# An encoder layer on one core: four pairs of seven per block instead of three, and their recombination as accumulating DMAs on GpSimd's queue

## The chip, the core and the metric

The kernel runs on one core of one Trainium2 chip. A core has TensorE (PE in the rows, with its weight loads as PEld), VectorE (DVE), ScalarE (ACT), GpSimd (POOL) and SyncE (SP), and 16 DMA engines that move data for the queues of SP, ACT and POOL. The metric is the device time of one execution in microseconds (us), and the time of a kernel is the median of its runs. Lower is better.

## What is computed

One layer: a feed-forward half step, a mixing stage (a Fourier branch and a recurrent branch, gated and merged), a second feed-forward half step, and a final RMS norm. All data are float32, 256 positions of 2048 features, and the inner width of the feed-forward is 5632. The change concerns the two feed-forwards:

```
def swiglu(h, w_gate, w_up, w_down):
    return (jax.nn.silu(h @ w_gate) * (h @ w_up)) @ w_down
...
h = rms_norm(x, ffn1_norm[l])
x = x + FFN_RES_SCALE * swiglu(h, ffn1_w_gate[l], ffn1_w_up[l], ffn1_w_down[l])
...
h = rms_norm(x, ffn2_norm[l])
x = x + FFN_RES_SCALE * swiglu(h, ffn2_w_gate[l], ffn2_w_up[l], ffn2_w_down[l])
```

## The kernel before

**Precision.** A float32 operand is split into a high part (ACT casts it, `whi` at line 157) and a low part (DVE subtracts, `wlo` at line 158). A product then takes three matmuls: high by high, high by low, low by high.

**Gate/up.** Each feed-forward first computes gate and up in 11 blocks (NB) of 512 columns. A block walks over the 2048 input features in 8 pairs of 256; each pair needs one chunk of 1 MB of weights, four tiles of 128x512 (up and gate, two halves of 128 features each). The four output banks of a block are gate and up for two halves of the 256 positions. A pair is done in one of two ways. With **eight** products (24 matmuls of 512 columns) it needs only the four tiles' high and low parts. With **seven** products (Strassen's scheme in Winograd's form, 21 matmuls) it needs sums and differences of the weight tiles (`t13`, `t24` and their high and low parts, lines 172 to 190, nine buffers) and of the activations (`sm`, from `Norm.sums`). The seven products go to seven PSUM banks (P1 to P7), which at the end of a block are copied out by ACT (line 390, into `ga`, `gd`, `gb`, `gc`, `xt`) and then **recombined** by five additions on DVE (lines 398 to 404). SiLU (ACT, lines 402 and 406), the product gate times up (DVE, lines 407 and 409), and eight transposes on PE with a copy and a store on ACT's DMA queue (`turn`, lines 413 to 421: `gt`, then `dn`) follow. Of the 11 blocks the first has no seven, the other ten have three, in the order E S E S E S E E (E for eight, S for seven).

**Order.** Weights are prepared two pairs ahead (LOOK = 2): while PE works on pair n, ACT and DVE prepare pair n + 2. The recombination of block b - 1 stands in the program behind the preparation in pairs 1 to 4 of block b (`combine(b - 1, n - 1)`, lines 463 and 464), and its `turn` in pair 1 of block b + 1. Inside a feed-forward `keep_order` holds every engine to the program's order.

**Buffers.** The pool `unit` (30 buffers of 4 KB a partition) holds the activations, `sm`, `ga` to `gc`, and all tiles of the preparation by seven; a tile takes over the buffer of a tile that was released, and waits for the last reader of that one. Raw weights have three buffers (`raw`), loaded by SP in order; a load waits until the preparation of the chunk that held the buffer is done. The residual `x` has 16 KB a partition of its own.

**Down.** Then comes the down projection over 88 groups of 8 weight tiles. Its input G is read back from DRAM (`gf`, SP's queue, line 475) and split (lines 298 and 299) during the first 22 groups, two groups for each block of gate/up; the recombination of the last block is run there too, by the hooks `ahead(t)` at groups 2t:

```
dn_hooks = dict(dn_hooks) | {2 * t: ahead(t) for t in range(NB)}
```

## Time and profile before

| | |
|---|---|
| median of 3 runs | 1980.38 us (1977.99 to 1981.15) |
| the profiled execution's own time | 1980.42 us |
| its span in the trace | 1978.6 us |
| PE busy | 1959.8 us, 99% of the span |
| DVE, ACT, POOL busy | 1464.2, 1145.8, 0.2 us |
| granted TensorE clock, mean | 0.996 |
| DMA | 400.80 MB, mean 203 GB/s |

The span runs from the first to the last instruction that the trace shows; the time has 1.8 us more, for what lies around it. A matmul's end is modelled, so the busy share of PE is not its efficiency; the time from one start to the next is what counts.

### The profile page before, as it was taken

To read this page: it belongs to the slowest core of one execution; us is meant where nothing else is said; L and a number is where in the kernel's file an instruction comes from. 1 tells how busy PE (TensorE), PEld (TensorE's weight loads), DVE (VectorE), ACT (ScalarE), POOL (GpSimd) and SP (SyncE) were. 2 spreads that over 40 slices of the span, in tenths; PEclk is the share of its full clock that TensorE was granted. 3 is DMA by queue.
4 is the path that set the end of the run, shared out by engine and by line. 5 is a ranking of instruction groups with operands and counts; after the bars stand their busy time and mean duration, and the time that the engine had idled before them with its cause. 6 is when DMAs were issued, how large, how long until landed. Compare 5 with 4: busy or idle time off the path is not lost.

```text
span 1978.6 us, 25578 instructions
## 1 busy us (share of the span) xinstructions
PE 1959.8 (99%) x10196; PEld 1679.7 (85%) x10196; DVE 1464.2 (74%) x1657; ACT 1145.8 (58%) x1491; POOL 0.2 (0%) x4
## 2 busy tenths in 40 slices
PE   9999999999999999999999999999999999999997
PEld 7888888888888888898888888888888888888887
DVE  7898888888665557755886767778888888855454
ACT  7666566666554445558965555566656666654442
POOL 0000000000000000000000000000000000000000
PEclk9999999999999999999999999999999999999998
DMA  7666566666754555445555555646656666665462
GB/s 266 208 211 217 199 209 215 212 212 235 266 211 154 215 189 200 171 170 183 182 190 190 192 191 187 218 170 213 202 203 213 219 217 213 238 242 211 153 222 94
DMA packets 61143, 400.80 MB, mean 203 GB/s; under 512 B 7008, under 2 KB 7648, under 8 KB 16352
## 3 DMA queue, kind: packets, MB, share of 16 engines
q1 hardware_dynamic: 57168, 387.04, 56.5%
q10 hardware_dynamic: 3856, 12.13, 1.5%
q8 instruction: 79, 1.29, 0.3%
q14 instruction: 40, 0.33, 0.0%
HBM read 385.52 MB, written 13.63 MB: 202 GB/s over the span
## 4 chain that ended last, share of the span: by engine, by line
PE 96%; DVE 2%; ACT 1%; issue 0%; DMA 0%; SPq 0%; DVEq 0%; ACTq 0%
PE ps L448 45%; PE ps L227 31%; PE ps L232 17%; PE ps L417 1%; PE ps L229 1%; PE ps L230 1%; DVE lo L187 0%; DVE wlo L158 0%; ACT whi L157 0%; PE ps L692 0%; DMA x<-xT 0%; DVE x L901 0%; DVE gb L400 0%; DVE ga L398 0%; PE ps L705 0%
## 5 line engine op out<-in xcount | busy, mean ns | idle before, releaser
L158 DVE TENSOR_TENSOR wlo<-raw,whi 128x1024 fp32r<-128x1024 f32 (+1 forms) x589 | 702.2, 1220 | 318.2 <-ACT whi L157 317.4
L157 ACT CAST whi<-raw 128x1024 fp32r<-128x1024 f32 (+1 forms) x589 | 596.8, 1047 | 349.6 <-PE ps L227 260.3
L448 PE MATMUL ps<-whi,m 128*128 128x512 f32 x1856 | 583.4, 390 | 1.2 <-ACT whi L157 1.1
L448 PEld LDWEIGHTS ps<-whi,m 128*128 128x128 f32 x1856 | 349.1, 188 | 74.4 <-ACT whi L157 1.9
L448 PE MATMUL ps<-wlo,m 128*128 128x512 f32 x928 | 362.1, 390 | 0.5 <-DVE wlo L158 0.5
L227 PE MATMUL ps<-G,whi 128*128 128x512 f32 x1320 | 332.7, 394 | 4.8 <-ACT whi L157 4.0
L227 PEld LDWEIGHTS ps<-G,whi 128*128 128x128 f32 x1320 | 237.9, 189 | 49.1 <-ACT whi L157 4.6
L227 PE MATMUL ps<-m,whi 128*128 128x512 f32 x896 | 225.4, 393 | 0.0
L448 PEld LDWEIGHTS ps<-wlo,m 128*128 128x128 f32 x928 | 174.5, 188 | 37.4 <-DVE wlo L158 1.1
L232 PEld LDWEIGHTS ps<-G,wlo 128*128 128x128 f32 x1408 | 191.9, 191 | 13.0
L232 PE MATMUL ps<-G,wlo 128*128 128x256 f32 x1408 | 196.8, 283 | 0.0
L227 PEld LDWEIGHTS ps<-m,whi 128*128 128x128 f32 x896 | 160.9, 189 | 28.5
L182 ACT CAST t24h<-t 128x1024 fp32r<-128x1024 f32 x60 | 63.3, 1055 | 123.3 <-DVE t L178 123.3
L232 PEld LDWEIGHTS ps<-m,wlo 128*128 128x128 f32 x896 | 122.2, 190 | 8.4
L232 PE MATMUL ps<-m,wlo 128*128 128x256 f32 x896 | 125.6, 282 | 0.0
L448 PE MATMUL ps<-bh,m 128*128 128x512 f32 x240 | 95.1, 396 | 0.0
L187 DVE TENSOR_TENSOR lo<-t,t24h 128x1024 fp32r<-128x1024 f32 x60 | 73.3, 1221 | 21.7 <-ACT t24h L182 21.7
L448 PE MATMUL ps<-t13h,sm 128*128 128x512 f32 x240 | 83.7, 389 | 0.0
L187 DVE TENSOR_TENSOR lo<-raw,bh 128x1024 fp32r<-128x1024 f32 x60 | 73.1, 1219 | 0.0
L187 DVE TENSOR_TENSOR lo<-t,t13h 128x1024 fp32r<-128x1024 f32 x60 | 73.1, 1219 | 0.0
L176 DVE TENSOR_TENSOR t<-raw 128x1024 f32<-128x1024 f32 x60 | 73.1, 1218 | 0.0
L448 PE MATMUL ps<-lo,m 128*128 128x512 f32 x180 | 70.4, 391 | 0.1
(207 smaller groups left out, 2098.5 us busy)
## 6 DMA issues: line engine op xcount, KB each, us to landing
raw<-gu SPq DMA_DIRECT2D x171, 1024.0 KB, 4.9
raw<-dn SPq DMA_DIRECT2D x88, 1024.0 KB, 5.1
raw<-gates_w SPq DMA_DIRECT2D x34, 1024.0 KB, 4.9
raw<-win SPq DMA_DIRECT2D x24, 1024.0 KB, 5.0
raw<-proj SPq DMA_DIRECT2D x16, 1024.0 KB, 4.9
raw<-wout SPq DMA_DIRECT2D x16, 1024.0 KB, 4.9
dn<-gt ACTq DMA_DIRECT2D x22, 512.0 KB, 3.6
gf<-dn SPq DMA_DIRECT2D x22, 512.0 KB, 6.3
```

The lines of the kernel that those rows point to most:

```text
L157: ACT.copy(hi[:, a:b, :], src[:, a:b, :])
L158: DVE.tensor_tensor(lo[:, a:b, :], src[:, a:b, :], hi[:, a:b, :].bitcast(F32), ALU.subtract)
L176: DVE.tensor_tensor(t13, r[:, 0:4:3, :], r[:, 1::-1, :], ALU.subtract)
L182: ACT.copy(t24h, t24)
L187: DVE.tensor_tensor(lo, src, hi.bitcast(F32), ALU.subtract)
L227: PE.matmul(o[:, 0:512], lhsT=w, rhs=mv(0, 512), start=first, stop=False)
L229: PE.matmul(o[:, 0:256], lhsT=w, rhs=mv(0, 256), start=first, stop=False)
L230: PE.matmul(o[:, 0:256], lhsT=w, rhs=mv(256, 512), start=False, stop=False)
L232: PE.matmul(o[:, 0:256], lhsT=lo[:, t * P:(t + 1) * P], rhs=mv(0, 256), start=False, stop=last)
L417: PE.transpose(o[:, j // 2, 256 * (j % 2) + P * h:256 * (j % 2) + P * (h + 1)], g[:, h, P * j:P * (j + 1)], ident)
L448: PE.matmul(bank[o], lhsT=lhs, rhs=rhs, start=o not in begun, stop=left[o] == 0 and k == 2)
```

## The change

- `SPLIT` goes from three to four pairs of seven in each block but the first, and the order of a block becomes E S E S E S E S, so that a block ends with a seven. In every block but the first of each feed-forward one pair of 24 matmuls becomes one of 21.
- The five additions of the recombination leave DVE and become five DMAs on POOL's queue with an accumulating add (`add_to`): one operand is read, and added to the target in SBUF. The third reads what the first wrote, the fourth and the fifth read what the third wrote.
- The recombination now starts in pair 0 of the next block, in five steps instead of four; SiLU stays in pairs 2 and 3.
- `x` loses its own memory and becomes four tiles of the pool `unit`, which goes from 30 to 35 buffers. `x.put` writes it to DRAM at pair 6 of the second gate/up, and `x.get` is given to the down projections as a hook at group 14.
- `Norm.sums(3)` of the first feed-forward moves from pair 16 to pair 8.

```
--- before.py
+++ after.py
@@ -26,7 +26,7 @@
 
 NB = F // 512
 
-SPLIT = [0] + [3] * 10
+SPLIT = [0]+[4]*10
 
 
 GROUPS_DN = [(2, 4)] + [(1, KF)] * (KD // 2 - 2)
@@ -75,14 +75,13 @@
 
     const = ctx.enter_context(tc.tile_pool(name="const", bufs=1))
     wraw = ctx.enter_context(tc.tile_pool(name="wraw", bufs=3))
-    unit = ctx.enter_context(tc.tile_pool(name="unit", bufs=30))
+    unit = ctx.enter_context(tc.tile_pool(name="unit", bufs=35))
     wspl = ctx.enter_context(tc.tile_pool(name="wspl", bufs=8))
     work = ctx.enter_context(tc.tile_pool(name="work", bufs=2))
     psum = ctx.enter_context(tc.tile_pool(name="psum", bufs=4, space=bass.MemoryType.PSUM))
     dram = ctx.enter_context(tc.tile_pool(name="dram", bufs=1, space=bass.MemoryType.DRAM))
 
 
-    x = const.tile([P, KD, T], F32, name="x")
     pr = const.tile([P, NPAR], F32, name="pr")
     ones = const.tile([P, P], F32, name="ones")
     DVE.memset(ones, 1.0)
@@ -94,6 +93,33 @@
 
     def unit_tile(dt, shape=(P, 2, 512), name="u"):
         return unit.tile(list(shape), dt, tag="u", name=name)
+
+    class Residual:
+
+
+        def __init__(self):
+            self.new()
+
+        def new(self):
+            self.tiles = [unit_tile(F32, (P, 4, T), name="x") for _ in range(KD // 4)]
+
+        def __getitem__(self, key):
+            p, k, t = key
+            if isinstance(k, int):
+                return self.tiles[k // 4][p, k % 4, t]
+            assert k.start // 4 == (k.stop - 1) // 4
+            return self.tiles[k.start // 4][p, k.start % 4:k.start % 4 + k.stop - k.start, t]
+
+        def put(self, to):
+            for i, t in enumerate(self.tiles):
+                SP.dma_start(to[:, 4 * i:4 * i + 4, :], t)
+
+        def get(self, src):
+            self.new()
+            for i, t in enumerate(self.tiles):
+                SP.dma_start(t, src[:, 4 * i:4 * i + 4, :])
+
+    x = Residual()
 
     def new_ps():
         return psum.tile([P, 2, 512], F32, tag="ps", name="ps")
@@ -361,7 +387,7 @@
 
         def combine(b, n):
             g = late[0](n)
-            if n == 3:
+            if n == 4:
                 late.pop(0)
                 ready.append((b, g))
 
@@ -376,8 +402,8 @@
                 def rest(step):
                     if step < 2:
                         ACT.activation(a[:, step, :], a[:, step, :], AF.Silu, scale=norm.cols[:, step:step + 1])
-                    if step > 1:
-                        i = step - 2
+                    if step > 2:
+                        i = step - 3
                         DVE.scalar_tensor_tensor(g[:, i, :], d[:, i, :], norm.cols[:, i:i + 1], a[:, i, :], ALU.mult, ALU.mult)
                     return g
                 return evict, rest
@@ -389,20 +415,24 @@
             def evict(n):
                 ACT.copy(to[n], bank[n])
 
+            def add_to(o, t):
+                nc.gpsimd.dma_start(o, t, accum_op=ALU.add)
+
             def both(t):
                 return t.to_broadcast([P, 2, 512])
 
             def rest(step):
 
                 if step == 0:
-                    DVE.tensor_tensor(a, a, both(g[:, 0:1, :]), ALU.add)
-                    DVE.tensor_tensor(xt, xt, c[:, 1, :], ALU.add)
-                    DVE.tensor_tensor(g, c, both(a[:, 1:2, :]), ALU.add)
+                    add_to(a, both(g[:, 0:1, :]))
+                    add_to(xt, c[:, 1, :])
+                    add_to(c, both(a[:, 1:2, :]))
                 elif step == 1:
+                    add_to(d, c)
+                    add_to(xt, c[:, 0, :])
+                elif step == 2:
                     ACT.activation(a[:, 0, :], a[:, 0, :], AF.Silu, scale=R[:, 0:1])
-                    DVE.tensor_tensor(d, d, g, ALU.add)
-                    DVE.tensor_tensor(xt, xt, g[:, 0, :], ALU.add)
-                elif step == 2:
+                elif step == 3:
                     ACT.activation(d[:, 0, :], d[:, 0, :], AF.Silu, scale=R[:, 1:2])
                     DVE.scalar_tensor_tensor(g[:, 0, :], d[:, 1, :], R[:, 0:1], a[:, 0, :], ALU.mult, ALU.mult)
                 else:
@@ -460,8 +490,8 @@
                     del full[:k]
                 prep_upto(q + LOOK, lambda: empty(EARLY))
                 empty(8)
-                if b and 0 < n < 5:
-                    combine(b - 1, n - 1)
+                if b and n < 5:
+                    combine(b - 1, n)
         return lambda n: combine(NB - 1, n), lambda: turn(*ready.pop(0))
 
     def ffn(gu_nm, dn_nm, norm, after, cols_at, hooks={}, last=None, dn_hooks={}):
@@ -486,9 +516,9 @@
 
         def ahead(t):
             def run():
-                if t < 4:
+                if t < 5:
                     combine(t)
-                if t in (1, 4):
+                if t in (1, 5):
                     turn()
                 load_g(t + 2)
                 split_g(t + 1)
@@ -841,10 +871,10 @@
         return lambda: [f(j) for j in js]
     hooks = {0: each(n1.moving, [2, 3]), 1: each(n1.moving, [4, 5]), 2: each(n1.moving, [6]), 3: each(n1.moving, [7]),
              4: each(n1.square, range(3)), 5: each(n1.square, range(3, 6)), 6: each(n1.square, range(6, 8)),
-             7: lambda: ACT.dma_start(ident, eye), 16: each(n1.sums, [3])}
+             7: lambda: ACT.dma_start(ident, eye), 8: each(n1.sums, [3])}
     hooks |= {k: (lambda k=k, h=h: (h(), n1.sums(k - 3))) for k, h in list(hooks.items()) if 3 <= k <= 5}
     nm = Norm(C_GM)
-    ffn("gu1", "dn1", n1, nm.tile_ready, 8, hooks, dn_hooks={30: decay})
+    ffn("gu1", "dn1", n1, nm.tile_ready, 8, hooks, dn_hooks={14: lambda: x.get(xT), 30: decay})
     n2 = Norm(C_G2)
     mix(nm, n2.tile_ready)
 
@@ -885,8 +915,9 @@
         add_sums(acc[:, 0, :], True, False)
         add_sums(acc[:, 1, :], False, False)
 
-    ffn("gu2", "dn2", n2, final_pair, 2, {2 + p: (lambda p=p: n2.sums(p)) for p in range(4)}, last=final_last,
-        dn_hooks={86: sums_so_far})
+    xd = dram.tile([P, KD, T], F32, name="xd")
+    ffn("gu2", "dn2", n2, final_pair, 2, {2 + p: (lambda p=p: n2.sums(p)) for p in range(4)} | {6: lambda: x.put(xd)},
+        last=final_last, dn_hooks={14: lambda: x.get(xd), 86: sums_so_far})
     tot = sums[0]
     y = work.tile([P, 2], F32, tag="sm2", name="sm2", bufs=1)
     root_columns(tot, y)
```

**POOL.** Before, POOL's queue holds no DMA. These are two blocks' recombinations in the changed program (line 419 is `add_to`; the names in brackets are the semaphores that an instruction waits for, DMASW for those of POOL's own DMAs, Activation for ACT's copies out of PSUM). The numbers tell the buffers apart.

```order
L419 DMA ga_1876<-gb_1878 128x2x512 [waits DVE_49,DMAHW5_49,PE_49,Activation_49]
L419 DMA xt_1880<-gc_1879 128x512 [waits DMASW1_49,DMASW0_49,Activation_49]
L419 DMA gc_1879<-ga_1876 128x2x512 [waits DMASW0_49,DVE_49,DMASW7_49,PE_49,Activation_49]
L419 DMA gd_1877<-gc_1879 128x1024 [waits DMASW1_49]
L419 DMA xt_1880<-gc_1879 128x512
L419 DMA ga_2217<-gb_2219 128x2x512 [waits DVE_49,DMAHW6_49,PE_49,Activation_49]
L419 DMA xt_2221<-gc_2220 128x512 [waits DMASW6_49,DMASW5_49,Activation_49]
L419 DMA gc_2220<-ga_2217 128x2x512 [waits DMASW4_49,DVE_49,DMASW5_49,PE_49,Activation_49]
L419 DMA gd_2218<-gc_2220 128x1024 [waits DMASW6_49]
L419 DMA xt_2221<-gc_2220 128x512
```

What is new is a chain of three DMAs of 512 KB, each behind the landing of the one before (`ga`, then `gc`, then `gd`), and two of 256 KB beside it.

**DVE.** Around the preparation of pair 5 of a block, the program before has on DVE (`lo` is the low part of a tile of the seven, line 187; `gb<-gd` is the product gate times up):

```order
L398 TENSOR_TENSOR ga_1769<-ga_1769,gb_1771 128x1024
L399 TENSOR_TENSOR xt_1773<-xt_1773,gc_1772 128x512
L400 TENSOR_TENSOR gb_1771<-gc_1772,ga_1769 128x1024 [waits DVE_49]
L158 TENSOR_TENSOR wlo_1990<-raw_1896,whi_1989 128x1024 [waits DMAHW5_49,Activation_49]
L158 TENSOR_TENSOR wlo_1994<-raw_1896,whi_1993 128x1024 [waits Activation_49]
L403 TENSOR_TENSOR gd_1770<-gd_1770,gb_1771 128x1024 [waits DVE_49]
L404 TENSOR_TENSOR xt_1773<-xt_1773,gb_1771 128x512
L176 TENSOR_TENSOR t13_2027<-raw_1938 128x1024 [waits DMAHW6_49,PE_49]
L177 TENSOR_TENSOR t24_2028<-raw_1938,t13_2027 128x512 [waits DVE_49,PE_49]
L178 TENSOR_TENSOR t24_2028<-raw_1938,t24_2028 128x512 [waits DVE_49]
L184 TENSOR_TENSOR b22_2024<-raw_1938,b22_2024 128x512 [waits Activation_49]
L187 TENSOR_TENSOR lo_2037<-raw_1938,bh_2023 128x1024 [waits PE_49]
```

and the changed program at the same place (lines 202 to 213 are 176 to 187 of before, line 437 is 407):

```order
L202 TENSOR_TENSOR t13_2066<-raw_1980 128x1024 [waits DMAHW6_49,PE_49]
L203 TENSOR_TENSOR t24_2067<-raw_1980,t13_2066 128x512 [waits DVE_49,PE_49]
L204 TENSOR_TENSOR t24_2067<-raw_1980,t24_2067 128x512 [waits DVE_49]
L210 TENSOR_TENSOR b22_2063<-raw_1980,b22_2063 128x512 [waits Activation_49]
L213 TENSOR_TENSOR lo_2076<-raw_1980,bh_2062 128x1024 [waits DMASW2_49,DMASW3_49,DMASW1_49,DMASW0_49]
L213 TENSOR_TENSOR lo_2078<-t24_2067,t24h_2064 128x1024 [waits PE_49,Activation_49]
L213 TENSOR_TENSOR lo_2080<-t13_2066,t13h_2065 128x1024 [waits Activation_49]
L437 SCALAR_TENSOR_TENSOR gb_1878<-gd_1877,cols0_554,ga_1876 128x512 [waits DMASW7_49]
```

The five additions are gone, and the first `lo` of pair 5 now waits for the last four of the five DMAs of the block before, the third, fourth and fifth among them: it takes the buffer of that block's `gc`.

**SP.** In the first feed-forward's end and on to the second's start, SP's queue of the changed program reads (line 175 loads weights, line 505 loads `gf`, line 115 is `x.put`):

```order
L505 DMA gf<-dn_10_153 128x1024
L175 DMA raw<-dn 128x2048 x32
L175 DMA raw<-win 128x2048 x24
L175 DMA raw<-gates_w 128x2048 x34
L175 DMA raw<-proj 128x2048 x16
L175 DMA raw<-wout 128x2048 x16
L175 DMA raw<-gu 128x2048 x10
L115 DMA xd<-x 128x1024 x4
L175 DMA raw<-gu 128x2048 x78
```

Four stores of `x` (512 KB each) are new. No load of `x` stands in the down projection, here or in the second one: the hook at group 14 has the key of `ahead(7)`, and the merge of the two tables keeps `ahead(7)`. So `x` stays in its four tiles of `unit` throughout, and 31 of the 35 buffers are left for the rest.

## Rows read from the trace of the kernel before

**Rows 1.** The page: span and busy time.

```profile
span 1978.6 us, 25578 instructions
...
PE 1959.8 (99%) x10196; PEld 1679.7 (85%) x10196; DVE 1464.2 (74%) x1657; ACT 1145.8 (58%) x1491; POOL 0.2 (0%) x4
```

**Rows 2.** The page's chain that ended last, shares of the span by line.

```profile
PE ps L448 45%; PE ps L227 31%; PE ps L232 17%; PE ps L417 1%; PE ps L229 1%; PE ps L230 1%; DVE lo L187 0%; DVE wlo L158 0%; ACT whi L157 0%; PE ps L692 0%; DMA x<-xT 0%; DVE x L901 0%; DVE gb L400 0%; DVE ga L398 0%; PE ps L705 0%
```

**Rows 3.** That chain in order of time, gate/up: start, length, what.

```profile
189.47 41.56 PE ps L448 x183
231.03 0.87 PE ps L417 x8
231.90 41.56 PE ps L448 x183
```

**Rows 4.** Windows: length, busy time of each engine, clock, DMA share, GB/s.

```profile
231.90:274.30 42.40, 42.40 (x193) 35.07 (x192) 37.12 (x39) 26.33 (x33) 0.00 (x0) 1.00 0.62 211
478.10:505.80 27.70, 27.29 (x161) 23.80 (x161) 22.16 (x26) 18.74 (x26) 0.00 (x0) 1.00 0.75 274
505.80:533.70 27.90, 27.90 (x161) 24.55 (x160) 17.54 (x19) 14.20 (x19) 0.00 (x0) 1.00 0.84 293
```

**Rows 5.** DVE, one block of gate/up: start, length, line, idle before.

```profile
238.98 1.22 DVE L398 TENSOR_TENSOR ga<-ga,gb 128x1024 f32<-128x1024 f32 x1
...
241.85 2.35 DVE L158 TENSOR_TENSOR wlo<-raw,whi 128x1024 fp32r<-128x1024 f32 x2
244.12 1.22 DVE L403 TENSOR_TENSOR gd<-gd,gb 128x1024 f32<-128x1024 f32 x1
...
245.86 1.22 DVE L176 TENSOR_TENSOR t<-raw 128x1024 f32<-128x1024 f32 x1
...
249.12 1.22 DVE L187 TENSOR_TENSOR lo<-raw,bh 128x1024 fp32r<-128x1024 f32 x1
...
252.52 0.75 DVE L407 SCALAR_TENSOR_TENSOR gb<-gd,cols,ga 128x512 f32<-128x512 f32 x1
```

**Rows 6.** PE, the same block: the first matmuls of pair 5.

```profile
250.12 0.84 PE L448 MATMUL ps<-b,sm 128*128 128x512 f32 x3
```

**Rows 7.** ACT, the same block: copies of two banks out of PSUM.

```profile
255.95 1.07 ACT L390 COPY gc<-ps 128x512 f32<-128x512 f32 x2
```

**Rows 8.** Groups, 147.06 to 443.9 us: line, shapes, count, busy us, mean ns.

```profile
L157 ACT CAST whi<-raw 128x1024 fp32r<-128x1024 f32 x70 | 69.3, 1050 | 18.5 <-PE ps L448 18.5
...
L182 ACT CAST t24h<-t 128x1024 fp32r<-128x1024 f32 x21 | 22.2, 1055 | 43.9 <-DVE t L178 43.9
...
L175 ACT CAST b<-raw 128x512 fp32r<-128x512 f32 x21 | 12.9, 615 | 0.0
```

**Rows 9.** SP's waits, 189.4 to 274.3 us: total, times, longest.

```profile
SPq L149 <- DVE wlo L158: 46.6, 10, 7.0
SPq L149 <- DVE lo L187: 38.0, 7, 6.2
```

**Rows 10.** The page's DMA issues: count, KB each, median us to landing.

```profile
raw<-gu SPq DMA_DIRECT2D x171, 1024.0 KB, 4.9
...
dn<-gt ACTq DMA_DIRECT2D x22, 512.0 KB, 3.6
gf<-dn SPq DMA_DIRECT2D x22, 512.0 KB, 6.3
```

**Rows 11.** Line 475 (`gf<-dn`), the same three figures of its 22 DMAs.

```profile
DMA to landing us min/median/max: 5.7/6.3/9.4
```

**Rows 12.** What PE waited for, whole run: total us, times, longest.

```profile
PE ps L227 <- DVE G L299: 0.8, 2, 0.4
```

**Rows 13.** DVE, start of the first down projection: a split of G.

```profile
493.68 1.29 DVE L299 TENSOR_TENSOR G<-gf,G 128x512 fp32r<-128x512 f32 x2
```

**Rows 14.** The chain there: PE's group that uses this G.

```profile
496.51 1.84 PE ps L227 x8
```

**Rows 15.** What ACT waited for, 478 to 560 us: total, times, longest.

```profile
ACT G L298 <- DMA gf<-dn: 19.5, 7, 4.3
```

## The prediction

> **What bounds the kernel now.** I read the page first: PE is busy for 1959.8 of 1978.6 us [rows 1], and the chain that ended last lies on PE's matmuls almost alone, 45% of the span on line 448, the matmuls of gate/up [rows 2]. The reader should then look at that chain in order of time. One block of gate/up is 183 matmuls in 41.56 us and eight transposes in 0.87 us, and the next block starts at once [rows 3]: 0.2271 us a matmul, a period of 42.43 us, no gap. So in gate/up the time is the number of matmuls, as long as ACT, DVE and the DMAs keep up. The windows say how close that is: in a block of 42.40 us DVE is busy 37.12 us, ACT 26.33 us, the DMA engines 0.62 of the time, at the full granted clock [rows 4].
>
> **What is saved on PE.** Ten blocks in each of two feed-forwards lose 24 - 21 = 3 matmuls: 60 x 0.2271 = 13.6 us. Nothing stands in for them, since PE has no wait there.
>
> **DVE.** In DVE's timeline the distance between starts gives the net cost. Preparing an eight takes 244.12 - 241.85 = 2.27 us, a seven 252.52 - 245.86 = 6.66 us [rows 5], so the fourth seven adds 4.39 us a block. The five additions go: from 238.98 to 241.85 and from 244.12 to 245.86, 4.61 us [rows 5]. DVE gets 0.22 us less work in a block that is 0.68 us shorter: 36.9 of 41.75 us. It stays just below saturation; cost nothing, and the cover is its idle time, 4.8 us a block against 5.3 before.
>
> **ACT.** A seven costs three casts of 1.05 us and one of 0.62 us, an eight two of 1.05 us [rows 8]: 1.7 us more in a block, 28.0 of 41.75 us. Hidden. The copies of P1, P6, P5 and P7 move from the block's middle to its end, behind the others, since the last pair is now a seven. PE needs these banks again one pair later (24 matmuls, 5.4 us) and a copy takes about 0.5 us [rows 7]; the other four banks are complete after 9 of the 21 matmuls, earlier than before. Nothing.
>
> **The accumulating DMAs.** This is the unknown: the trace has no DMA from POOL and no accumulate. Call L the time from one link of the chain (`ga`, `gc`, `gd`) being free to start until it has landed. What the chain delays first is not SiLU but the first `lo` of pair 5, which takes the buffer of `gc`; behind it on DVE stand the rest of pair 5, the product gate times up and the preparations of pairs 6 and 7, and PE waits for these. Deadline: in the block before, this `lo` started at 249.12, and PE began pair 5 at 250.12 and did not wait [rows 5, 6]. Pairs 0 to 4 are 24 + 21 + 24 + 21 + 24 = 114 matmuls, with the transposes 26.8 us, so that block began at 223.4 and the `lo` may start 25.7 us into a block. The chain starts when ACT has copied P6: after the block's end come the copies of P1 and P6, with what is left of the casts before them some 1.5 us. So 1.5 + 3L <= 25.7: L may be up to **8.1 us**. Beyond it each us of L costs 3 us in each of 18 blocks (the chain of the last block of a feed-forward runs in the down projection), since the deadline moves with the block: 54 us.
>
> Bounds for L, from transfers of the same 512 KB: 3.6 us (`dn<-gt`, ACT's queue) below; 9.4 us, the longest of `gf<-dn` in SP's queue beside the weights, above [rows 10, 11]. I take the median of `gf<-dn`, 6.3 us: an accumulate moves the bytes of the target too, so it is nearest to a 512 KB transfer that shares the engines with others, and 1 MB of weights lands in 4.9 us [rows 10]. Then the chain ends 1.5 + 18.9 = 20.4 us into the block, 5 us early. Cost nothing; at 9.4 us it ends at 29.7, 4.0 us late, 72 us in 18 blocks.
>
> For the price of a link there is a page: the Trainium skill, DMA: Bandwidth & Descriptors, section Anatomy of one DMA, fits a DMA of GpSimd's queue as 2.0 us plus the bytes at 436 GB/s. That would make an estimate of 3.2 us for 512 KB, 4.4 us if the target's bytes count as well, and the chain would be hidden, the sum unchanged.
>
> A rule that speaks against the change has to be weighed here. DVE is busy 37.12 of 42.40 us, and its additions take 1.22 us for 1024 columns, more than 1 ns a column [rows 4, 5]. The Trainium skill, SBUF — State Buffer, section SBUF: two separate sides, warns that a DVE instruction in a two-port mode keeps GpSimd from writing descriptors until it ends. The same page lists two-input tensor_tensor as having no such mode, and the durations agree. If each link did wait for one DVE instruction, L would be 1.2 us more, 7.5 us, and the chain would end at 24.0 us, still in time; but the slack would be nearly gone. This is one reason why the chance of a late chain is not small.
>
> **The weights.** SP waits in these two blocks 46.6 + 38.0 = 84.6 of 84.9 us for DVE to free a raw buffer [rows 9]; loads are never what is late. Between the issue of a load and its use DVE prepares two pairs, 6.66 + 2.27 = 8.9 us, and a load lands in 4.9 us [rows 5, 10]: 4 us of slack. The accumulates add 2 MB a block, 4 MB if the target counts twice: 48 or 96 GB/s on top of 211 at a share of 0.62, so 0.76 to 0.90. Hidden, with loads some us longer.
>
> **The change of buffers and x.** `x` is never reloaded and so never leaves SBUF; 31 buffers are left where 30 were. One seven more needs no more at a time, as sevens are still two pairs apart. The second gate/up gets four stores of `x`, 2 MB in its first block, which has no sevens and so a lightly loaded DVE: nothing. What would have been freed is not, and the wait of `lo` for `gc` above is its price.
>
> **Start of the down projections.** Before, PE waits twice 0.4 us for a split of G on DVE [rows 12], behind three of the five additions. These are gone: -0.8 us. Against it, here the DMAs are already at 0.75 to 0.84 (274 to 293 GB/s) [rows 4], and the last block's accumulates, 2 to 4 MB over some 20 us, would take them to full. ACT already waits 19.5 us for `gf` [rows 15]. A split of G ends at 493.68 + 1.29 = 494.97, and PE uses it at 496.51 [rows 13, 14]: 1.5 us of slack. If `gf` comes 2 to 3 us later for three of the splits while the chain runs, PE waits 0.5 to 1.5 us for each: 1.5 to 4.5 us in each feed-forward; none if `gf` stays within its slack, 6 at most. I take 2 us each: +4 us.
>
> **Sum.** 1980.4 - 13.6 - 0.8 + 4 = 1970.0 us. The working goes by the profiled execution, whose time of 1980.42 us is the median's (1980.38) within 0.1 us, so nothing is corrected.
>
> **Rivals.**
> - *The chain is late (slower).* L above 8.1 us: descriptors made by software, two reads for each write, packets of 2 KB that queue behind the weights' larger ones. For it: the deadline leaves 1.8 us a link, and `gf<-dn` at its longest is over it [rows 11]. Against it: the same view's median is far under it. At 54 us for each us, L = 8.5 gives 1970 + 22 = 1992, L = 9.4 gives 2042. From L = 8.3 us on it eats the whole gain.
> - *The weights are late.* Accumulates and loads share the 16 engines, and a load takes over 8.9 us. The Trainium skill, DMA: Bandwidth & Descriptors, section Issuing engines are not separate DMA queues, says that DMAs of all queues run on the same engines and interleave; the 0.62 above is measured without such a mix. It needs loads 1.8 times as long; at 10 us in two pairs of each block, 2 x 1.1 x 20 = 44 us: about 2014.
> - *The gain is lost at the down projections and in small waits.* 6 us in each down start, and 0.1 us a block where DVE comes just in time: 1980.4 - 13.6 - 0.8 + 12 + 2 = 1980, no change.
> - *The change doesn't do what it says.* That holds for `x`, as shown; it costs nothing by itself, and the matmuls go either way.
>
> **Chances.** The forecast (chain hidden) 0.62, chain late 0.22, weights late 0.08, gain lost 0.08. A measurement of this kernel tells about 0.2% (4 us) from no change. The forecast's own range is 1965 to 1977: 1966 without contention at the down start, 1978 with the most of it, so 0.05 of its 0.62 falls within 0.2%. Faster 0.58 (the forecast but for these 0.05, and 0.01 of the others); same 0.13 (0.05, the 0.08 of the lost gain); slower 0.29. The range of 8 in 10 goes from 1964 to 2012: little lies below, as PE has no more to give than 14.4 us, and above it stay a chain with L over 8.8 us and the worse half of the late weights, under 0.2.
>
> **What would show it.** In gate/up of the changed kernel the chain in order of time should show 180 matmuls in 40.9 us and no pieces of DVE or POOL between blocks; a link from issue to landing should be 5 to 8 us, and `lo` in pair 5 should not wait for a DMA. The prediction is wrong if PE waits there for `lo` and DVE for `gd<-gc` (the first rival), if ACT or DVE wait for `raw` (the second), or if G's split waits for `gf` by more than before.

## The result and the profile after

The changed kernel takes 2127.6 us against 1980.0: a ratio of 1.0737 (1.0724 to 1.0750), 147.6 us slower. The prediction was 1970, with a range up to 2012.

The page of the changed kernel, the span, the engines and the chain that ended last by line (they answer to [rows 1, 2]):

```profile
span 2125.9 us, 25832 instructions
...
PE 1991.7 (94%) x10136; PEld 1694.4 (80%) x10136; DVE 1457.5 (69%) x1657; ACT 1176.4 (55%) x1532; POOL 103.5 (5%) x104
...
PE ps L253 29%; PE ps L478 22%; PE ps L258 16%; DMA gc<-ga 10%; DMA xt<-gc 5%; DVE lo L213 1%; DMA gd<-gc 1%; DVE wlo L184 1%; DMA raw<-gu 1%; PE ps L255 1%; PE ps L256 1%; PE ps L447 1%; DVE t L202 1%; DMA gf<-dn 0%; ACT whi L183 0%
```

PE has 60 matmuls less and yet is busy for 32 us longer; and where the chain was PE alone, a sixth of it now is DMAs of the recombination. That chain in order of time, a piece of one block (answers to [rows 3]):

```profile
295.92 8.62 PE ps L478 x38
304.54 0.89 PE ps L447 x8
...
309.16 14.37 DMA gc<-ga
323.53 0.40 issue
323.93 0.55 POOL gd L419
324.48 5.42 DMA xt<-gc
329.90 0.02 issue
329.92 1.24 DVE lo L213
331.16 0.04 issue
331.20 5.07 PE ps L478 x11
```

The last accumulate lands, `lo` starts 0.02 us later, PE 0.04 us after `lo`: a hand-over without slack. The five accumulates of this block on POOL (start, length of the issue, what; in brackets the idle time before):

```profile
301.04 1.20 POOL L419 DMA_DIRECT2D ga<-gb  x1 [26.37 <-ACT ga L416]
301.76 1.42 POOL L419 DMA_DIRECT2D xt<-gc  x1
309.16 1.21 POOL L419 DMA_DIRECT2D gc<-ga  x1 [5.97 <-DVE b L210]
323.93 0.90 POOL L419 DMA_DIRECT2D gd<-gc  x1 [13.55 <-DMA gc<-ga]
324.48 1.24 POOL L419 DMA_DIRECT2D xt<-gc  x1
```

Call C the time from the issue of `ga` to the landing of the second `xt`, here 324.48 + 5.42 - 301.04 = 28.9 us. Its legs are 8.1 us (`gc` overwrites what the first `xt` reads, so it waits for that landing too, here at 301.76 + 6.72 = 308.48; it is issued some 0.7 us after it in every block, so the `DVE b` that the view names as last is not what releases it), 14.8 and 6.0. The next `ga` is issued at 352.02, so the period, from one `ga` to the next, is 51.0 us. Over six blocks of the first gate/up (from the `ga` at 151.41 to that at 451.76) C is 27.9 us and the period 50.06 us.

The windows of this block (length, busy time of PE, its weight loads, DVE, ACT, POOL, granted clock, DMA share, GB/s; [rows 4] has a block of before):

```profile
301.00:323.90 22.90, 22.90 (x107) 18.95 (x106) 15.01 (x16) 13.19 (x16) 3.36 (x3) 1.00 0.85 258
323.90:331.20 7.30, 0.83 (x4) 0.36 (x3) 1.28 (x2) 2.66 (x4) 1.80 (x2) 0.91 0.59 109
331.20:335.00 3.80, 3.80 (x9) 2.98 (x10) 3.80 (x4) 1.42 (x2) 0.00 (x0) 0.50 0.77 248
335.00:340.00 5.00, 5.00 (x19) 4.04 (x19) 4.86 (x7) 0.24 (x1) 0.00 (x0) 0.83 0.52 193
```

PE stands for 6.5 of the 7.3 us, and DVE stands with it. Behind the gap the granted clock is 0.50, the 1.2 GHz level: 9 matmuls in 3.8 us. Over the whole run PE waits for these (total us, times, longest), and DVE for this one:

```profile
PE ps L478 <- DVE lo L213: 90.6, 18, 7.6
PE ps L253 <- DVE G L325: 14.9, 3, 7.2
PE ps L478 <- ACT m L331: 5.5, 1, 5.5
```

```profile
DVE lo L213 <- DMA xt<-gc: 168.9, 16, 12.6
```

DVE waits longer than PE, up to 12.6 us in a block where it had 5 us to spare [rows 4]. And the DMAs by form (count, KB, median us to landing; [rows 10]):

```profile
raw<-gu SPq DMA_DIRECT2D x171, 1024.0 KB, 4.9
...
gf<-dn SPq DMA_DIRECT2D x22, 512.0 KB, 7.1
ga<-gb POOLq DMA_DIRECT2D x20, 512.0 KB, 6.0
xt<-gc POOLq DMA_DIRECT2D x40, 256.0 KB, 6.7
gc<-ga POOLq DMA_DIRECT2D x20, 512.0 KB, 12.4
gd<-gc POOLq DMA_DIRECT2D x20, 512.0 KB, 4.6
```

### The profile page after: what moved, and what is told of

The parts are those of the page before. It is cut to its first block, busy times and chain, and to the rows that moved or that the text cites. A ratio compares the mean times of both kernels' runs of the same rounds, so it can differ in the third digit from the quotient of the medians.

```text
span 2125.9 us, 25832 instructions
## 1 busy us (share of the span) xinstructions
PE 1991.7 (94%) x10136; PEld 1694.4 (80%) x10136; DVE 1457.5 (69%) x1657; ACT 1176.4 (55%) x1532; POOL 103.5 (5%) x104
## 3 DMA queue, kind: packets, MB, share of 16 engines
q0 software_dynamic: 19520, 41.95, 10.9%
## 4 chain that ended last, share of the span: by engine, by line
PE 69%; DMA 18%; issue 5%; DVE 5%; ACT 3%; POOL 1%; ACTq 0%; SPq 0%; DVEq 0%; POOLq 0%
PE ps L253 29%; PE ps L478 22%; PE ps L258 16%; DMA gc<-ga 10%; DMA xt<-gc 5%; DVE lo L213 1%; DMA gd<-gc 1%; DVE wlo L184 1%; DMA raw<-gu 1%; PE ps L255 1%; PE ps L256 1%; PE ps L447 1%; DVE t L202 1%; DMA gf<-dn 0%; ACT whi L183 0%
## 5 line engine op out<-in xcount | busy, mean ns | idle before, releaser
L184 DVE TENSOR_TENSOR wlo<-raw,whi 128x1024 fp32r<-128x1024 f32 (+1 forms) x549 | 655.1, 1219 | 285.2 <-ACT whi L183 284.5
L183 ACT CAST whi<-raw 128x1024 fp32r<-128x1024 f32 (+1 forms) x549 | 558.8, 1047 | 298.7 <-PE ps L253 268.1
L478 PE MATMUL ps<-whi,m 128*128 128x512 f32 x1536 | 491.0, 392 | 10.3 <-ACT m L331 5.5
L253 PE MATMUL ps<-G,whi 128*128 128x512 f32 x1320 | 336.0, 397 | 18.9 <-DVE G L325 14.9
L478 PEld LDWEIGHTS ps<-whi,m 128*128 128x128 f32 x1536 | 290.5, 189 | 73.2 <-ACT m L331 5.8
L478 PE MATMUL ps<-wlo,m 128*128 128x512 f32 x768 | 301.3, 392 | 1.7 <-DVE wlo L184 1.7
L213 DVE TENSOR_TENSOR lo<-raw,bh 128x1024 fp32r<-128x1024 f32 x80 | 97.6, 1220 | 168.9 <-DMA xt<-gc 168.9
L258 PEld LDWEIGHTS ps<-G,wlo 128*128 128x128 f32 x1408 | 192.7, 192 | 13.1
L478 PE MATMUL ps<-lo,m 128*128 128x512 f32 x240 | 106.3, 443 | 90.6 <-DVE lo L213 90.6
L478 PEld LDWEIGHTS ps<-lo,m 128*128 128x128 f32 x240 | 49.9, 208 | 109.7 <-DVE lo L213 101.5
L478 PE MATMUL ps<-bh,m 128*128 128x512 f32 x320 | 136.0, 425 | 0.0
L478 PE MATMUL ps<-t13h,sm 128*128 128x512 f32 x320 | 113.3, 395 | 0.0
L200 ACT CAST bh<-raw 128x1024 fp32r<-128x1024 f32 x80 | 83.8, 1048 | 39.3 <-DMA raw<-gu 28.9
```

Of the source, the lines that this page charges most:

```text
L183: ACT.copy(hi[:, a:b, :], src[:, a:b, :])
L184: DVE.tensor_tensor(lo[:, a:b, :], src[:, a:b, :], hi[:, a:b, :].bitcast(F32), ALU.subtract)
L200: ACT.copy(b13, r[:, 1:3, :])
L213: DVE.tensor_tensor(lo, src, hi.bitcast(F32), ALU.subtract)
L253: PE.matmul(o[:, 0:512], lhsT=w, rhs=mv(0, 512), start=first, stop=False)
L258: PE.matmul(o[:, 0:256], lhsT=lo[:, t * P:(t + 1) * P], rhs=mv(0, 256), start=False, stop=last)
```

## The experiments

The theory to start with: the chain is late because its second link shares the DMA engines with the weights. Rivals: the accumulate itself is slow, wherever it runs; descriptors made on POOL are slow; the fourth seven costs the time; the buffer of `gc` alone is to blame; the drop of the clock is to blame.

**1. The price of an accumulate by itself.** A kernel that only moves data, with one DMA at a time, alone or started together with one or two weight loads. Two of its forms:

```
+    def rows2(t, u):
+        nc.gpsimd.dma_start(t, u[:, 0:1, :].to_broadcast([P, 2, 512]), accum_op=ALU.add)
...
+    def copy4(t, u):
+        nc.gpsimd.dma_start(t, u)
```

> This kernel computes nothing of the reference: it only moves data, one DMA after the other, each behind the landing of the one before, alone and with one or two weight loads of 1 MB started at the same moment. Seven forms, six of each: accumulate 512 KB in rows of 2 KB (the form of ga and gc), accumulate 512 KB in rows of 4 KB (gd), accumulate 256 KB in rows of 2 KB (xt), plain copies of the first two on POOL's queue, a plain copy of 512 KB on ACT's queue, accumulate 1 MB in rows of 8 KB. Theory (a link is slow because it shares the DMA engines with weights whose packets are four times larger): alone 4 to 5 us for 512 KB, beside two loads 10 to 14 us, plain copies on POOL's queue nearly as slow as accumulates beside loads, rows of 8 KB hardly slowed beside loads. Rival 1 (the accumulate itself is slow): alone already 6 us or more, a plain copy 3 to 4 us alone and at most 6 us beside two loads. Rival 2 (descriptors made on POOL are slow): rows of 4 KB, with half the packets, take nearly half the time of rows of 2 KB, alone and beside loads, accumulate or not.

Median us to landing, six of each:

| form | alone | beside 1 MB | beside 2 x 1 MB |
|---|---|---|---|
| accumulate 512 KB, rows of 2 KB | 5.0 | 8.6 | 10.4 |
| accumulate 512 KB, rows of 4 KB | 4.5 | 8.8 | 10.4 |
| accumulate 256 KB, rows of 2 KB | 3.3 | 7.0 | 8.9 |
| accumulate 1 MB, rows of 8 KB | 6.9 | 11.4 | 13.1 |
| copy 512 KB, POOL's queue, rows of 2 KB read | 3.1 | 7.1 | 8.9 |
| copy 512 KB, POOL's queue, rows of 4 KB | 2.9 | 7.0 | 8.9 |
| copy 512 KB, ACT's queue, rows of 4 KB | 2.9 | 4.9 | 8.9 |

The stretches of accumulates and copies of 512 KB, each six of them alone (length, busy DVE and POOL, clock, DMA share, GB/s):

```profile
25.86:60.00 34.14, 1.95 (x19) 7.42 (x6) 1.00 0.54 92
184.49:215.80 31.31, 1.95 (x19) 5.23 (x6) 1.00 0.53 100
471.50:494.30 22.80, 1.96 (x19) 4.41 (x7) 1.00 0.36 138
599.71:621.00 21.29, 1.95 (x19) 3.24 (x6) 1.00 0.36 148
```

The first two rows are accumulates, in rows of 2 and of 4 KB, the others copies. An accumulate holds the 16 engines for 0.54 x 34.14 / 6 = 3.1 us, in rows of 4 KB for 0.53 x 31.31 / 6 = 2.8; a copy for 0.36 x 22.80 / 6 = 1.4 and 0.36 x 21.29 / 6 = 1.3. So it takes 2.2 times the engine time, 1.6 to 1.9 us more to landing when alone. Rows of 8 KB are slowed by the loads as much as rows of 2 KB: the packets' size, on which my theory rested, is not it, and rows of 2 against 4 KB make 0.5 us alone and nothing beside two loads, so neither is the number of descriptors. POOL's queue has a part beside one load, where the same copy lands 2.1 us earlier on ACT's queue; alone and beside two loads the two are equal. (The copy that reads rows of 2 KB moves in packets of 4 KB, like the other copy.) But one link alone, at 5 us, is still cheaper than the 6.3 us that the prediction took.

**2. The matmuls alone.** The kernel before with one line changed (and the sums of the fourth seven made earlier, as in the change):

```
-SPLIT = [0] + [3] * 10
+SPLIT = [0]+[4]*10
```

> The matmul part of the change by itself: the kernel before with four pairs of seven, all five additions still on DVE, x still in its own memory. The prediction's term for the matmuls is -13.6 us: 1966 us if DVE keeps up. DVE's work by the rows of before is 37.12 us a block plus 4.39 us for the fourth seven, 41.5 us of a block of 41.75, so it may be the bound: up to 1975 us then. The rival, by which the fourth seven (its casts, its differences, its buffers) is what costs the time, expects over 2000 us.

1984.2 us, a ratio of 1.0016 (1.0007 to 1.0026): PE's saving is lost. A window of gate/up:

```profile
350.00:392.00 42.00, 41.87 (x187) 33.86 (x186) 40.64 (x43) 27.23 (x35) 0.00 (x0) 1.00 0.60 206
```

DVE is busy for 40.6 of 42.0 us, and the period is 42.58 us where PE alone would need 41.7: DVE is the bound there, and more tightly than "up to 1975" allowed. So something has to leave DVE, or the fourth seven gains nothing.

**3. The chain alone.** The changed kernel with three sevens:

```
-SPLIT = [0]+[4]*10
+SPLIT = [0]+[3]*10
```

> The accumulating DMAs by themselves: the changed kernel with three pairs of seven as before. Theory (the chain is late, whatever the number of sevens): the loss of the changed kernel against its saving, 2127.6 - (1980.0 - 13.6) = 161 us, comes back nearly whole, less where the lighter DVE catches up: 2090 to 2140 us, with lo of the sixth pair waiting for the landing of the last accumulate in 16 blocks. Rival (the fourth seven is what costs): 1980 us within 10.

2043.0 us, a ratio of 1.0319 (1.0295 to 1.0343), with the wait of `lo` for `xt<-gc` in 16 blocks (110.7 us in sum, where it was 168.9). Neither theory's number, but one between them. C is as long as in the changed kernel (28.8 us in the first gate/up), but the period is 44.9 us, C and 16.1 us. The same chain costs less here; the chain's end cannot be all that counts. Behind that `lo` DVE has two eights to prepare here, in the changed kernel an eight and a seven, 4.4 us more [rows 5].

**4. Copies in place of the accumulates.** The sums of the recombination are left out.

```
-                nc.gpsimd.dma_start(o, t, accum_op=ALU.add)
+                nc.gpsimd.dma_start(o, t)
```

> The changed kernel with the five accumulating DMAs as plain copies of the same operands on the same queue: the recombination is left out (the target is overwritten instead of added to), everything else is as in the changed kernel. Theory (packets of 2 KB behind the weights' packets of 8 KB): a copy has as many packets, so the second link stays at 10 us or more and the time at 2060 to 2130 us. Rival (reading and adding the target is what makes a link slow): links of 4 to 6 us, no wait of lo, 1966 to 1985 us.

1972.2 us, a ratio of 0.9962 (0.9946 to 0.9977). The rival holds, and no copy takes the 10 us of the theory: the medians are 5.0 us for `ga`, 5.7 for `gc`, 5.0 for `gd`. Against packets by themselves this run says less than was expected of it, since the copies of `ga`, `gc` and `xt` move in packets of 4 KB where the accumulates' have 2 KB (11840 packets on POOL's queue, where the changed kernel has 19520); there run 1 decides, by accumulates with packets of both sizes. The profiled execution, one of the longer ones (1980.3 us; the ten lie between 1968.0 and 1981.8), shows more. In its second gate/up C is 18.7 us and the period 41.73, the one that PE alone would need. In its first C is 21.2 and the period 43.4, with waits of `lo`. Between the two the chain begins to cost. A block of the second:

```profile
1506.58 0.71 POOL L419 DMA_DIRECT2D ga<-gb  x1 [28.18 <-ACT ga L416]
1507.29 0.56 POOL L419 DMA_DIRECT2D xt<-gc  x1
1512.94 0.73 POOL L419 DMA_DIRECT2D gc<-ga  x1 [5.10 <-PE ps L478]
1518.61 0.55 POOL L419 DMA_DIRECT2D gd<-gc  x1 [4.94 <-DMA gc<-ga]
1519.15 0.54 POOL L419 DMA_DIRECT2D xt<-gc  x1
```

and its `lo`, which waits for 1 us:

```profile
1525.92 1.23 DVE L213 TENSOR_TENSOR lo<-raw,bh 128x1024 fp32r<-128x1024 f32 x1 [0.99 <-DMA xt<-gc]
```

**5 and 6. Smaller loads beside the chain.** `Half` stands for `r` in the preparations and gives the first half of it for either half.

```
+                if 8 <= c < 88 or len(chunks) - 176 <= c < len(chunks) - 88:
+                    SP.dma_start(r[:, 0:8 * P], chunks[c][:, 0:8 * P])
+                else:
+                    SP.dma_start(r, chunks[c])
```

> The changed kernel with weight loads of gate/up of half the size: from the ninth load of each feed-forward on, 512 KB instead of 1 MB, and the preparations read the half twice, so half of the weights is left out; the work of PE, DVE and ACT and the accumulates are as in the changed kernel. In the micro-kernel an accumulate of 512 KB lands after 5.0 us alone, 8.6 beside one load of 1 MB and 10.4 beside two. Theory (accumulates are long because they take twice a copy's time on the engines and share these with the weights): the chain from the first issue to the last landing falls from 28.9 us to 18 to 22, lo of the sixth pair hardly waits, 1964 to 1990 us. Rival (the chain's length comes from the accumulates and their waits for each other alone): 25 us or more, over 2060 us.

2058.2 us, a ratio of 1.039 (1.0369 to 1.0412). The edit's condition was not what the text above says: of the second gate/up it halved the loads of the first 44 pairs only, and 44 loads of the mixing stage with them. The second edit has `len(chunks) - 132 <= c < len(chunks) - 44` there: it halves the loads of the first gate/up from the ninth on and all of the second, and none elsewhere:

> The run with half-sized weight loads again, set right: the run before it halved the loads of the first gate/up (from the ninth on), but of the second only those of its first 44 pairs, and 44 loads of the mixing stage. Here all loads of both gate/ups but the first eight are halved, and none elsewhere (half of these weights is left out). In the earlier run the blocks with halved loads had a chain of 21.8 us and a period of 43.95 us, those of the changed kernel 27.8 and 50.06. Theory (the loads beside the chain lengthen it by 6 us; the period is the chain's length and some 22 us of work on DVE and PE behind it): 18 blocks x 2.2 us over 41.75, some 14 us at the starts of the down projections, 3 at the start: 1967 + 40 + 17 = 2024, 2010 to 2035 us. Rival (the second gate/up is late for another reason than the loads): 2045 us or more, as in the earlier run.

2028.1 us, a ratio of 1.0238 (1.022 to 1.0255), inside the range. A block of it:

```profile
324.51 1.21 POOL L436 DMA_DIRECT2D ga<-gb  x1 [26.27 <-ACT ga L433]
...
333.14 1.22 POOL L436 DMA_DIRECT2D gc<-ga  x1 [6.49 <-ACT t13h L213]
339.88 0.91 POOL L436 DMA_DIRECT2D gd<-gc  x1 [5.52 <-DMA gc<-ga]
```

The leg of `gc` is 6.7 us where it was 14.8, its median to landing 7.3 us where it was 12.4. The loads do lengthen the chain, from 21.8 to 27.9 us on the average. But with 21.8 us, 26 us into the block, the chain still costs 2.3 us a block: the deadline of the prediction would have let it pass nearly free. The blocks of four runs with four sevens and the wait of `lo` in the same place, side by side (means over six or seven blocks of one gate/up):

| run | C | period | period - C |
|---|---|---|---|
| copies, second gate/up | 18.7 | 41.73 | (PE's own 41.7) |
| copies, first gate/up | 21.2 | 43.4 | 22.2 |
| loads halved, first gate/up | 21.8 | 44.04 | 22.2 |
| changed kernel, first gate/up | 27.9 | 50.06 | 22.2 |

Each microsecond of C makes the block one longer, and 22.2 us stay. That holds for each block by itself: in the changed kernel the distance from one `ga` to the next is C and 22.1 to 22.3 us in 16 of 18 cases, the other two being the last of each gate/up (43.8 and 43.9 us). The 22.2 us are what stands between the landing and the next issue of `ga`; in the block shown above, where it is at 329.90, on DVE, ACT and POOL:

```profile
336.93 1.21 DVE L202 TENSOR_TENSOR t<-raw 128x1024 f32<-128x1024 f32 x1
343.60 2.35 DVE L184 TENSOR_TENSOR wlo<-raw,whi 128x1024 fp32r<-128x1024 f32 x2
347.91 0.69 DVE L204 TENSOR_TENSOR t<-raw,t 128x512 f32<-128x512 f32 x1
```

```profile
348.64 1.06 ACT L208 CAST t24h<-t 128x1024 fp32r<-128x1024 f32 x1 [1.58 <-DVE t L204]
351.02 0.60 ACT L416 COPY ga<-ps 128x512 f32<-128x512 f32 x1
```

```profile
352.02 1.21 POOL L419 DMA_DIRECT2D ga<-gb  x1 [26.30 <-ACT ga L416]
```

DVE works without a gap: the three `lo` of pair 5, both products and the preparation of an eight, then that of a seven (from 336.93), of the next block's first eight (from 343.60), and the differences of its first seven (to 348.60). ACT's two casts of these wait for DVE, and the copies of P1 and P6 (`ga`) stand behind them and start the next chain. PE is not on this way: it began the next block at 347.96, 3 us before the copy of P6. It is a loop, through the DMAs, DVE and ACT, and it is hidden only while C + 22.2 is below PE's 41.7 us: C up to **19.5 us**.

**7 and 8. Another buffer, later readers.** First x really leaves SBUF, so that `lo` takes another buffer:

```
-dn_hooks={14: lambda: x.get(xT), 30: decay}
+dn_hooks={15: lambda: x.get(xT), 30: decay}
...
```

The hook of the second feed-forward moves likewise.

> The changed kernel with the hook for x moved from group 14 to group 15, so that x does leave SBUF and four more buffers are free in gate/up: lo of the sixth pair then takes another buffer, and what waits first for the chain is SiLU of d on ACT (for gd) and, one pair later, b22 of the eighth pair. Theory (the end of the chain against its first reader is all that counts): gd lands about 1.4 us before xt and its reader is read by PE 4.8 us later than lo was, so the 7 us a block shrink to 1 to 3 us: 1990 to 2040 us. Rival (buffers do not matter, since SiLU waits for the same chain): 2110 to 2130 us. A third outcome, 1966 to 1975, would say that the buffer alone was the cause.

2083.3 us, a ratio of 1.051 (1.049 to 1.053). The gain of 44 us shows that the buffer was a part of it, but a smaller one than the theory had (1990 to 2040); now the wait stands elsewhere on ACT, and on DVE:

```profile
ACT gd L436 <- DMA gd<-gc: 178.8, 20, 12.7
```

```profile
DVE gb L437 <- DMA gd<-gc: 142.6, 20, 10.9
```

C is 28.8 us, the period 47.15: the loop is 18.3 us of work now, since its entry lies later in the block, and still C and this make more than 41.7. Then SiLU and the products two pairs later as well:

```
-                elif step == 2:
+                elif step == 4:
                     ACT.activation(a[:, 0, :], a[:, 0, :], AF.Silu, scale=R[:, 0:1])
...
```

> As the run before, and SiLU of d, both products and the transposes two pairs later (steps 4 to 6 instead of 2 to 4; SiLU of ga moves with them). Theory: the readers come 10 us later than in the changed kernel, more than the 7 us by which it is late, so nothing waits for the chain: 1964 to 1976 us. Rival (the accumulates also cost by delaying weights or by anything else than the wait at the chain's end): over 1985 us.

2058.4 us, a ratio of 1.0387 (1.0371 to 1.0402): a miss. Holding `ga`, `gd` and `gb` two pairs longer used the buffers up again, and the next in line for the buffer of `gc` is `b22` of the eighth pair, written by ACT:

```profile
ACT b L201 <- DMA xt<-gc: 148.4, 16, 11.6
```

C grew to 32 us and the period stayed at 46.8. A version with both later readers and enough buffers was not run, so whether the accumulates cost nothing once nobody reads them in time stays open.

**9 and 10. Only the first link by DMA.** `ga` and the first `xt` on POOL's queue, the other three additions on DVE in the third pair.

```
-                    add_to(c, both(a[:, 1:2, :]))
-                elif step == 1:
-                    add_to(d, c)
-                    add_to(xt, c[:, 0, :])
                 elif step == 2:
+                    DVE.tensor_tensor(c, c, both(a[:, 1:2, :]), ALU.add)
+                    DVE.tensor_tensor(d, d, c, ALU.add)
+                    DVE.tensor_tensor(xt, xt, c[:, 0, :], ALU.add)
...
```

> Four pairs of seven, the first link alone on POOL's queue (ga and the first xt, issued in the first pair of the next block); the other three additions on DVE in the third pair, the rest as in the changed kernel. DVE was busy 40.8 of 42.0 us of a block with all five additions on it; without these two (1.22 + 0.7 us) it is at 39 of 41.75. Theory: ga lands some 12 us into the block, DVE asks for it at 15 us or later, no wait: 1964 to 1972 us, under both kernels. Rival (any accumulate beside the weights costs, or DVE is still the bound): 1980 us or more.

1969.3 us, a ratio of 0.994 (0.9925 to 0.9955): 0.6% faster than the kernel before, as the theory expected. A block, and DVE's addition that reads the link:

```profile
400.00:441.70 41.70, 41.70 (x190) 34.49 (x189) 39.66 (x42) 27.71 (x35) 2.15 (x2) 1.00 0.72 234
```

```profile
408.03 1.22 DVE L430 TENSOR_TENSOR gc<-gc,ga 128x1024 f32<-128x1024 f32 x1
```

PE without a gap, the blocks 41.71 us apart, DVE at 39.7 of 41.7. The link was issued at 394.69 and had landed 7.0 us later, well before 408.03. The same with x back in its own memory:

```
-    unit = ctx.enter_context(tc.tile_pool(name="unit", bufs=35))
+    unit = ctx.enter_context(tc.tile_pool(name="unit", bufs=31))
...
+    x = const.tile([P, KD, T], F32, name="x")
...
-    x = Residual()
...
```

> As the run with only the first link on POOL's queue, and x back in its own memory (31 buffers for the rest, no store of x), so of the change only the fourth seven and the first link are left. There PE waited 4.8 us at the start for a product with x, which the kernel before does not. Theory: these 3 to 4 us come back: 1964 to 1967 us. Rival (that wait has another cause, or the stores of x cost nothing): 1968 to 1971 us.

1969.6 us, a ratio of 0.994 (0.9928 to 0.9952). The wait at the start is gone from the profile, the time is the same, the rival's number: moving x cost nothing that this measurement can tell. Its six times lie between 1965.8 and 1973.3 us, so a cost of 3 us could hide in them.

**11. PE kept busy in the gap.**

```
...
+                        if b > 1 and n == 5 and i == 1 and k == 0:
+                            for _ in range(28):
+                                PE.matmul(bank[o], lhsT=zero, rhs=norm.m[p][:, 0, :], start=False, stop=False)
...
```

> The changed kernel with 28 matmuls more (6.4 us at full clock) in the sixth pair of 18 blocks, ahead of the first matmul that waits for lo; they multiply with zeros, so they add nothing to the result. PE is then busy where it stood idle, and the granted clock should stay at 1.00. In the changed kernel's trace PE is idle 115 us longer than the matmul count accounts for and its matmuls are 45 us slower. Theory A (the slower matmuls behind each wait cost their 45 us): 2075 to 2100 us. Theory B (the period of a block is set by the loop through the chain and DVE, and PE at the lower clock has time): 2115 to 2135 us.

2117.6 us, a ratio of 1.0682 (1.0667 to 1.0696), 10 us less than the changed kernel. In the window that answers to the gap PE was busy and the clock stayed up; in the next one it shows 1.00 where the changed kernel had 0.50:

```profile
323.90:331.20 7.30, 7.22 (x32) 5.63 (x30) 0.24 (x1) 1.62 (x3) 1.80 (x2) 1.00 0.60 110
331.20:340.00 8.80, 7.59 (x32) 5.94 (x33) 8.68 (x9) 2.46 (x4) 0.00 (x0) 1.00 0.54 168
```

Theory B: the 45 us by which matmuls were slower do not come back. In the second window PE stands for 1.2 us and DVE for 0.1: the loop goes through DVE, and PE had time to be slow. The first gate/up, from its first to its last matmul, takes 534.6 us where it took 534.9, with the same C of 27.9 and the same 22.2 us behind it. The gain lies in the second, 520.2 against 528.6, where C was shorter in this execution (23.3 and 23.4 us in the first two blocks, 25.2 and 27.2 in the changed kernel); these two blocks took 48.06 us, close to what PE needs with 28 matmuls more. So a price of the clock is not shown; it is at most these 10 us.

**12. More memory for POOL's descriptors.** The data-moving kernel of run 1 again:

```
-    nc = bacc.Bacc("TRN2", target_bir_lowering=False, num_devices=1, dynamic_dma_scratch_size=1024)
+    nc = bacc.Bacc("TRN2", target_bir_lowering=False, num_devices=1, dynamic_dma_scratch_size=16384)
```

> The micro-kernel again, with 16 times the memory for the descriptors that POOL makes; it computes nothing of the reference. Rival (a link is slow because its 256 or 128 packets of 2 or 4 KB do not fit that memory at once, and POOL has to wait for it): accumulates of 512 KB fall from 5.0 and 4.5 us to 4 us or less alone, by as much beside loads. Theory (the accumulate itself holds the engines twice as long as a copy): 5.0 and 4.5 us alone, 10.4 us beside two loads, unchanged within 0.2 us.

Nothing changes: 5.0 and 4.5 us alone, 10.5 and 10.6 beside two loads. That rival falls for one DMA of POOL at a time; with two at once, as in the changed kernel, it was not tried.

## Why the prediction was wrong

- **Matmuls, -13.6 us: right.** With the first link alone on DMA the blocks are 41.71 us apart against 42.43 [rows 3]: 20 x 0.72 = 14.4 us.
- **DVE and ACT: right.** In the block from 301.04 to 352.02 of the changed kernel DVE is busy for 36.8 us (36.9 predicted), ACT for 27.9 (28.0). But the prediction didn't see what run 2 shows, that with four sevens the five additions cannot stay on DVE.
- **The deadline of the chain: the step that failed in the mechanism.** "The `lo` may start 25.7 us into a block" took the moment at which PE first reads `lo` as the limit, as if DVE could wait until then for nothing. What is queued behind that `lo` on DVE leads to the next issue of `ga`: with the 22.2 us of this loop C may be 19.5 us. The prediction allowed 25.7 - 1.5 = 24.2. The start of the chain was early as well: `ga` is issued 301.04 - 297.05 = 4.0 us into the block (the transposes at 304.54 stand behind 33 matmuls, 7.5 us), because the copy of P6 comes after two casts that wait for DVE.
- **L = 6.3 us: the term that was mis-sized, and what turned the sign.** C is 27.9 us, 9.3 us a link, just under the upper bound of 9.4. The reason given for 6.3, that an accumulate is like a transfer of its size beside others, comes near for copies (run 4: 5.0 to 5.7 us). An accumulate has 2.2 times a copy's engine time (run 1), and in this kernel the second link runs beside weight loads, two at a time, and a store (14.4 us in the block shown; a median of 12.4, and of 7.3 when the loads are halved). On this the estimate from the Trainium skill (DMA: Bandwidth & Descriptors, section Anatomy of one DMA) can be read again: 3.2 us for 512 KB agrees with a copy alone (2.9 to 3.1), 4.4 with the target's bytes counted is close to an accumulate alone (4.5 to 5.0), and both are far from the 12.4 us in place, which it does not speak of.
- **Together.** With the right deadline 6.3 us a link would have been hidden by 0.6 us, not by 5, so the deadline alone would not have cost anything. With the measured C and the prediction's deadline a block would have been 27.9 - 24.2 = 3.7 us late; with the loop it is 27.9 + 22.2 - 41.7 = 8.4 us. Over the 16 periods that follow this sum the mean is 49.90 us, so 16 x 8.2 = 131 us. The price in the prediction, 3 us a block for each us of L, was right, but in 16 blocks and not in 18: the last period of each gate/up is only some 2 us too long.
- **The rival "the chain is late" was the right mechanism**, and had a chance of 0.22; with L = 9.4 it gave 2042, since it had the same deadline. The other rival of DMAs, late weights, came only in part. The median of the loads is the same 4.9 us, but 29 of 182 took over 8.9 us, where 3 did before, and ACT waits 28.9 us in all for `raw<-gu` (17 times). By themselves these waits cost nothing that shows: in run 9 they are 35.8 us, and the blocks are 41.71 us.
- **POOL held up by DVE: not seen.** An issue of `ga` or `gc` takes 1.20 to 1.22 us on POOL in gate/up (the first 1.33), also where DVE subtracts throughout, and 1.21 to 1.23 in the kernel of run 1 (the first 1.33), where DVE has next to nothing to do. The rule of the Trainium skill (SBUF — State Buffer, section SBUF: two separate sides) had no place to act here.
- **Down projections, -0.8 + 4 us: too small.** PE waits 14.9 us for splits of G, against 0.8 [rows 12]; a `gf<-dn` takes up to 10.4 us, 9.4 before [rows 11]. In run 9, with two accumulates of the last block left, PE waits 2.5 us there.
- **x and the start.** PE waits 5.5 us for `m`, which is made from x; this was not foreseen. Run 10 shows no cost in the time, within its spread.
- **The clock** was not priced: at most 10 us, and none that is shown in the loop (run 11).

By the traces of the two kernels, from the first to the last matmul of each stage: the first gate/up takes 534.9 us where it took 471.3, the second 528.6 where it took 468.0. That is 124.2 us more although some 14 us of matmuls are gone, so 138 us were lost in the two, 131 and 4 of these in the periods just counted. What follows the two gate/ups takes 10.0 and 8.5 us longer, all of it before or behind the mixing stage, which takes 514.7 us in both kernels, and the start 4.4: 124.2 + 18.5 + 4.4 = 147.1 us of the 147.3 between the spans. The 18.5 us are only in part explained, by the 14 us of waits for G.

## What to carry to other kernels

When work moves from an engine into a chain of DMAs, don't compare its end with its first reader only: follow what is queued behind that reader round to the next start of the chain, and ask whether the loop, at the DMAs' length beside the other traffic, fits into the period. Price an accumulating DMA at twice a copy's engine time, as measured here, and let one link of a chain, with a third of a block from its issue to its reader, go by DMA before all of them do: here one link freed enough of DVE to make the fourth seven pay.

## What was unexpected of the hardware

- An accumulate within SBUF held the DMA engines 2.2 times as long as a copy of the same bytes (2.8 to 3.1 us against 1.3 to 1.4 for 512 KB); alone it landed in 4.5 to 5.0 us, beside two loads of 1 MB in 10.4.
- For accumulates the size of packets made no difference beside two loads: 512 KB in rows of 2 and of 4 KB both 10.4 us; 1 MB in rows of 8 KB took 13.1.
- A copy of 512 KB started together with one load landed in 7.0 us from POOL's queue and in 4.9 from ACT's; alone and beside two loads there was no difference.
- Behind the gap of 6.5 us on PE the granted clock was 0.50 in the next 3.8 us; with 28 matmuls by zeros in the gap it stayed at 1.00, and the kernel was no more than 10 us faster.
